# Other phased K pairs for each chunk pair of the input projection, corrected banks in another order, and the rotation on VectorE

## The chip, the cores and the metric

The kernel runs on one core of a Trainium2 chip. The metric is the device time of one execution in microseconds. Three timed runs of the kernel before took 2185.89, 2187.31 and 2187.89 us. Times inside an execution come from a trace of another run, whose zero is the start of its span.

## The reference

Two layers over 256 tokens of width 2048, all in float32. The stage that matters here is the input projection `proj = h @ w_in` and, on two of its six parts, the partial rotation.

```python
def hybrid_mixer(h, layer, w_in, w_o, ...):
    proj = h @ w_in                       # (256, 2048) @ (2048, 6144)
    q_sb, k_sb, v_sb, q_d, k_d, v_d = jnp.split(proj, offs.tolist(), axis=-1)
    o_sb = rms_norm(stick_breaking_attention(q_sb, k_sb, v_sb), sb_out_norm)
    q_d = partial_rope(q_d.reshape(b, s, DIFF_HEADS * 2, DIFF_QK_DIM), pos)
    k_d = partial_rope(k_d.reshape(b, s, DIFF_HEADS * 2, DIFF_QK_DIM), pos)
    o_d = rms_norm(differential_attention(q1, q2, k1, k2, v_d, lam), diff_subln) * (1.0 - lam_init)
    return jnp.concatenate([o_sb, o_d], axis=-1) @ w_o

def partial_rope(x, pos):                 # the first 16 of each 64 are turned, in halves of 8
    rot = jnp.concatenate([x1 * cos - x2 * sin, x2 * cos + x1 * sin], axis=-1)
    return jnp.concatenate([rot, x[..., ROT_DIM:]], axis=-1)

for l in range(DEPTH):
    x = x + rms_norm(hybrid_mixer(rms_norm(x, ...), ...), post_mix_norm[l])
    x = x + rms_norm(swiglu(rms_norm(x, ...), ...), post_ffn_norm[l])
```

## The kernel before

**Split products.** Each float32 matrix is split into a rounded part (hi) and its rest (lo). A product of two blocks is then three matmuls: hi with hi (L1240), hi of the activations with lo of the weights (L1241), and lo of the activations with hi of the weights (L1242). ScalarE (ACT) makes hi of the weights (L402, and in phased K pairs L350, L357 and L376), VectorE (DVE) makes lo (L341). There are six buffers each for hi and lo, and the weights come from HBM in the order in which they are used.

**The input projection.** The 6144 output columns are twelve chunks of 512. They are worked in six pairs of chunks, n = 0 to 5 (`PAIRS`), called pair 1 to pair 6 below. One pair has four banks of 128 tokens x 512 columns that gather in PSUM: two token tiles t0 and t1 for two chunks ca and cb. The code calls them x11 (t0, ca), x12 (t0, cb), x21 (t1, ca) and x22 (t1, cb). The 2048 rows of the weights are eight K pairs (kp), each with two tiles of 128 rows.

**Plain and phased K pairs.** A plain K pair takes eight block products, 24 matmuls (`eight_in`). A phased K pair takes seven, 21 matmuls (`phased`): a scheme of Strassen's kind in which sums of blocks are multiplied. It needs sums of the activations (the tiles `shin` and `slin`, made once for a K pair and layer by `pair_forms`) and sums of the weights, made on DVE for every chunk pair (L349, L351, L355 and L370), and gives seven products with the names g0, t1, t2, t3, then g1, b22, t4. In pair 1 all K pairs are plain. In pairs 2 to 6 the K pairs 0, 1 and 2 are phased (`IN_SEVEN`) and stand first; the plain ones 3 to 7 follow (`IN_PLAIN`). The three forms are made during pair 1.

**The correction.** After the first four products of each phased K pair the banks hold sums that must be set right once: ACT copies x11 (L1207, p1) and x21 (L1210, p7). DVE then makes v1 = x22 - p1 (L1213), x12 + v1 (L1216), x21 - v1 (L1217) and x22 = x12 - p7 (L1218). Only then can the last three products go on: g1 to x11, b22 to x12, t4 to x21. b22 also waits for L1218, which reads x12. The same `phased` serves one part of the output projection.

**The rotation.** `rotate` turns two chunks of q and two of k of the differential heads, for two token tiles: eight times a layer, on a tile of 128 x 128 elements each (8 heads of 16). It is four operations of GpSimd (POOL): L955 (times cosine), L956 and L957 (the exchanged halves times sine) and L958 (their sum). The tokens' rows come from ACT (L1089), and TensorE transposes the turned rows (L1107).

**What sets the order.** Each engine works through its own queue in order. A scheduler puts the instructions into these queues by priority and by what it expects of times; code under `high_priority(offset=URGENT)`, the correction among it, goes ahead of what else is ready. Attention work of finished chunks (`start(...)`) is fed in between the products of the later pairs.

Of the kernel before, what the change touches and what calls it, by code (L numbers as in the profile page):

```python
# [13 lines left out]
ALU = mybir.AluOpType  # L14
# [3 lines left out]
P = 128  # L18
# [4 lines left out]
KT = D // P  # L23
NH = 8
# [61 lines left out]
def weight_order():  # L86

    order = []

    def queue(*blocks):  # L90
        order.append(blocks)
        return len(order) - 1

    def queue_pair(name, l, kp, c):
        return queue((name, l, 2 * kp, c), (name, l, 2 * kp + 1, c))

    roles = {}
# [93 lines left out]
def kernel(  # L191
# [15 lines left out]
    nc = tc.nc  # L207
# [305 lines left out]
    rope_sb = const.tile([P, NT, 32], F32, name="rope_sb")  # L513
# [432 lines left out]
    def rotate(pool, tok, t, nm):  # L946
        v16 = tok.rearrange("p (h d) -> p h d", d=64)[:, :, 0:16]
        ra = pool.tile([P, NH, 16], F32, tag="ra", bufs=1, name=f"ra_{nm}")
        rb = pool.tile([P, NH, 16], F32, tag="rb", bufs=1, name=f"rb_{nm}")

        def table(a, b):
            return rope_sb[:, t, a:b].unsqueeze(1).to_broadcast([P, NH, b - a])

        eng = nc.gpsimd
        eng.tensor_tensor(out=ra, in0=v16, in1=table(0, 16), op=ALU.mult)  # L955
        eng.tensor_tensor(out=rb[:, :, 0:8], in0=v16[:, :, 8:16], in1=table(16, 24), op=ALU.mult)  # L956
        eng.tensor_tensor(out=rb[:, :, 8:16], in0=v16[:, :, 0:8], in1=table(24, 32), op=ALU.mult)  # L957
        eng.tensor_tensor(out=v16, in0=ra, in1=rb, op=ALU.add)  # L958

    def opening(pool, accs, xT, stats, sums_of, settle):  # L960

# [46 lines left out]
        for kp in range(KT // 2):  # L1008
            if kp:
                split(2 * kp)  # L1010
                split(2 * kp + 1)
            if kp + 2 < KT // 2:
                load()
                fetch(2 * kp + 6)
            for part in ((0,), (1,)) if kp == KT // 2 - 1 else (range(NT),):
                eight_in(accs, xT, 0, PAIRS[0], kp, part, kp == 0, kp == KT // 2 - 1, 0)
                if kp == KT // 2 - 1:
                    settle(part[0])
            if 3 <= kp < 7:
# [41 lines left out]
    def mixer_in(pool, l, rs, xT, mix, mixed, began):  # L1061
        heads = {}
        forms, forms_o = {}, {}
        mix_pool[0] = pool.sums

        def sums_of(kp):
            forms[kp] = pair_forms(pool, pool.sums, len(IN_SEVEN), xT, kp, f"in{l}")

        for n, cc in enumerate(PAIRS):
            banks = began[0] if n == 0 and began else four_banks(n == 0, [f"in{l}_{c}_{t}" for t in range(NT) for c in cc])  # L1070
# [50 lines left out]
                opening(pool, banks, xT, first_stats(pool, rs), sums_of, settle)  # L1121
                start(lambdas())
            else:
                kps = IN_PLAIN if n else range(KT // 2)
                ahead = list(KP_O[:2]) if alone else []
                if n:
                    open_sums[0] = True
                    w = pool.tile([P, 4, CW], F32, tag="gpost", bufs=1, name=f"w{l}_{n}")
                    phased(banks, forms, xT, ("in", l, n), IN_SEVEN, [w[:, i, :] for i in range(3)])
                for j, kp in enumerate(kps):  # L1130
                    last = j == len(kps) - 1
                    if n == 0 and 2 <= j < 2 + len(IN_SEVEN):
# [16 lines left out]
                    if ahead and heads[0, 1].keys() >= {"qdone", "kdone"}:  # L1149
                        kp = ahead.pop(0)  # L1150
# [11 lines left out]
    def phased(banks, sums, tiles, key, kps, w):  # L1162

        x11, x12, x21, x22 = banks
# [39 lines left out]
        p1, p7, v1 = w  # L1204
# [6 lines left out]
        products(z, "t2")  # L1211
        with tc.high_priority(offset=URGENT):
            nc.vector.tensor_tensor(out=v1, in0=x22, in1=p1, op=ALU.subtract)  # L1213
        products(z, "t1")
        with tc.high_priority(offset=URGENT):
            nc.vector.tensor_tensor(out=x12, in0=x12, in1=v1, op=ALU.add)  # L1216
            nc.vector.tensor_tensor(out=x21, in0=x21, in1=v1, op=ALU.subtract)  # L1217
            nc.vector.tensor_tensor(out=x22, in0=x12, in1=p7, op=ALU.subtract)  # L1218
# [162 lines left out]
    xT = None  # L1381
# [385 lines left out]
```

## Time and profile before

| what | value |
|---|---|
| three timed runs, median | 2187.31 us |
| the profiled execution | 2184.78 us |
| its span | 2183.0 us |
| its mean granted TensorE clock | 0.998 |
| pairs 2 to 6, layer 0 | 51.7 to 302.0 us |
| pairs 2 to 6, layer 1 | 1136.1 to 1390.0 us |

The profiled execution's own time is 1.8 us longer than the span of its instructions. The stage that the change touches takes some 250 us in each of the two layers. In a row of the trace, a line such as L341 names the line of the kernel that issued the instruction, and `out<-in` its tiles; 128x512 is partitions by elements.

### The profile page before, as it was taken

To read this page: it belongs to the slowest core of one execution; us is meant where nothing else is said; L and a number is where in the kernel's file an instruction comes from. 1 tells how busy PE (TensorE), PEld (TensorE's weight loads), DVE (VectorE), ACT (ScalarE), POOL (GpSimd) and SP (SyncE) were. 2 spreads that over 40 slices of the span, in tenths; PEclk is the share of its full clock that TensorE was granted. 3 is DMA by queue.
4 is the path that set the end of the run, shared out by engine and by line. 5 is a ranking of instruction groups with operands and counts; after the bars stand their busy time and mean duration, and the time that the engine had idled before them with its cause. 6 is when DMAs were issued, how large, how long until landed. Compare 5 with 4: busy or idle time off the path is not lost.

```text
span 2183.0 us, 28896 instructions
## 1 busy us (share of the span) xinstructions
PE 2161.0 (99%) x9902; PEld 1775.8 (81%) x9902; DVE 1979.1 (91%) x2725; ACT 1431.4 (66%) x2157; POOL 249.8 (11%) x238
## 2 busy tenths in 40 slices
PE   9999999999999999999999999999999999999998
PEld 7788888888888888888877778888888888888887
DVE  7988877899999999999898888778999999999997
ACT  7676765766666666666576667657666666676664
POOL 1200000021221220000020100000212212200000
PEclk9999999999999999999999999999999999999999
DMA  8544465487887876767454554655978878767673
GB/s 295 175 173 172 163 218 205 163 306 233 242 262 222 237 233 225 231 228 254 148 197 166 178 184 161 222 192 167 302 237 238 260 225 234 240 219 245 204 266 100
DMA packets 143443, 470.43 MB, mean 215 GB/s; under 512 B 16304, under 2 KB 17328, under 8 KB 142784
## 3 DMA queue, kind: packets, MB, share of 16 engines
q1 hardware_dynamic: 125120, 436.03, 57.3%
q0 software_dynamic: 17600, 32.02, 8.9%
q8 instruction: 77, 1.26, 0.2%
q14 instruction: 70, 0.57, 0.1%
q10 hardware_dynamic: 576, 0.54, 0.1%
HBM read 460.14 MB, written 8.39 MB: 215 GB/s over the span
## 4 chain that ended last, share of the span: by engine, by line
PE 89%; DVE 7%; issue 2%; DMA 1%; ACT 1%; SPq 0%; POOL 0%; DVEq 0%; ACTq 0%; POOLq 0%
PE c L1297 20%; PE in L1241 6%; PE in L1240 6%; PE in L1242 6%; PE dn L1615 4%; PE dn L1616 4%; PE dn L1618 4%; DVE lo L341 3%; PE p L1241 3%; PE c L1240 3%; PE c L1241 3%; PE p L1242 3%; PE c L1242 3%; PE p L1240 3%; PE o L690 2%; PE o L689 2%
## 5 line engine op out<-in xcount | busy, mean ns | idle before, releaser
L341 DVE TENSOR_TENSOR lo<-raw,hi 128x1024 fp32r<-128x1024 f32 (+1 forms) x512 | 597.7, 1186 | 75.8 <-ACT hi L402 49.0
L402 ACT ACTIVATE hi<-raw 128x1024 fp32r<-128x1024 f32 x444 | 455.8, 1057 | 112.4 <-DMA raw<-in_weights_in_turn_dram 64.0
L1297 PE MATMUL c<-hi,xF 128*128 128x512 f32 x1344 | 364.5, 392 | 0.5 <-DVE xF L603 0.5
L1297 PEld LDWEIGHTS c<-hi,xF 128*128 128x128 f32 x1344 | 249.7, 188 | 52.9 <-ACT act L1502 1.4
L296 POOL DMA_DIRECT2D T<-in_weights_in_turn_dram x122 | 107.8, 884 | 1355.9 <-DMA T<-in_weights_in_turn_dram 579.2
L1297 PE MATMUL c<-lo,xF 128*128 128x512 f32 x672 | 207.3, 390 | 0.0
L317 ACT ACTIVATE Th<-T 128x512 fp32r<-128x512 f32 x122 | 77.3, 633 | 193.0 <-DVE T L328 189.0
L317 ACT ACTIVATE Th<-G 128x1024 fp32r<-128x1024 f32 x122 | 129.2, 1059 | 81.7 <-DVE G L329 80.5
L1615 PE MATMUL dn<-hi,jh 128*128 128x512 f32 x416 | 162.0, 389 | 0.0
L1616 PE MATMUL dn<-lo,jh 128*128 128x512 f32 x416 | 161.8, 389 | 0.0
L319 DVE TENSOR_TENSOR Tl<-G,Th 128x1024 fp32r<-128x1024 f32 x122 | 149.2, 1223 | 11.6 <-ACT Th L317 11.6
L319 DVE TENSOR_TENSOR lo<-T,hi 128x1024 fp32r<-128x1024 f32 x122 | 155.1, 1271 | 0.1
L329 DVE TENSOR_TENSOR G<-G,T 128x1024 f32<-128x1024 f32 x122 | 149.0, 1221 | 4.9 <-POOL lo L405 3.1
L402 ACT ACTIVATE hi<-G 128x1024 fp32r<-128x1024 f32 x122 | 129.0, 1058 | 35.9 <-DMA G<-in_weights_in_turn_dram 18.7
L1297 PEld LDWEIGHTS c<-lo,xF 128*128 128x128 f32 x672 | 126.0, 188 | 26.4
L341 DVE TENSOR_TENSOR lo<-G,hi 128x1024 fp32r<-128x1024 f32 x104 | 127.1, 1222 | 10.6 <-ACT hi L402 10.5
L317 ACT ACTIVATE hi<-T 128x1024 fp32r<-128x1024 f32 x122 | 128.3, 1051 | 11.8 <-PE c L1242 8.3
L1618 PE MATMUL dn<-hi,jl 128*128 128x512 f32 x416 | 128.1, 389 | 0.0
L1240 PE MATMUL in<-hi,xT 128*128 128x512 f32 x309 | 123.1, 400 | 2.7 <-DVE in L1217 1.5
L1241 PE MATMUL in<-lo,xT 128*128 128x512 f32 x309 | 120.9, 392 | 0.5 <-DVE lo L1004 0.5
L1242 PE MATMUL in<-hi,xT 128*128 128x512 f32 x309 | 120.5, 390 | 0.0
L1240 PE MATMUL in<-hi,xI 128*128 128x512 f32 x285 | 114.3, 403 | 1.8 <-DVE in L1217 1.8
(462 smaller groups left out, 5057.3 us busy)
## 6 DMA issues: line engine op xcount, KB each, us to landing
raw<-in_weights_in_turn_dram SPq DMA_DIRECT2D x508, 512.0 KB, 4.8
T<-in_weights_in_turn_dram SPq DMA_DIRECT2D x122, 512.0 KB, 5.3
G<-in_weights_in_turn_dram SPq DMA_DIRECT2D x122, 512.0 KB, 5.4
T<-in_weights_in_turn_dram POOLq DMA_DIRECT2D x122, 256.0 KB, 5.8
u<-in_weights_in_turn_dram SPq DMA_DIRECT2D x34, 256.0 KB, 6.0
V<-in_weights_in_turn_dram SPq DMA_DIRECT2D x8, 512.0 KB, 4.4
away_ffn<-x SPq DMA_DIRECT2D x8, 512.0 KB, 7.2
xd<-away_ffn SPq DMA_DIRECT2D x8, 512.0 KB, 8.6
```

The source lines that it names most:

```text
L317: nc.scalar.activation(h, w, AF.Copy)
L319: newest_rest[i] = nc.vector.tensor_tensor(out=l, in0=w, in1=h.bitcast(F32), op=ALU.subtract)
L329: nc.vector.tensor_tensor(out=g, in0=g, in1=t2.unsqueeze(1).to_broadcast([P, 2, CW]), op=ALU.add)
L341: rests.append(nc.vector.tensor_tensor(out=lo, in0=src, in1=hi.bitcast(F32), op=ALU.subtract))
L402: nc.scalar.activation(hi, raw, AF.Copy)
L1240: nc.tensor.matmul(a, sh, hi, start=first, stop=False, skip_group_check=open_sums[0])
L1241: nc.tensor.matmul(a, sh, lo, start=False, stop=False, skip_group_check=open_sums[0])
L1242: return nc.tensor.matmul(a, sl, hi, start=False, stop=last, skip_group_check=open_sums[0])
L1297: nc.tensor.matmul(a, stat[part], w[j][:, kk, :], start=first and kk + n == 0, stop=last and kk == 1 and n == 2)
L1615: nc.tensor.matmul(accs[c, t], sh, hi[:, kk, :], start=first, stop=False, skip_group_check=open_sums[0])
L1616: nc.tensor.matmul(accs[c, t], sh, lo[:, kk, :], start=False, stop=False, skip_group_check=open_sums[0])
L1618: nc.tensor.matmul(accs[c, t], sl, hi[:, kk, :], start=False, stop=last, skip_group_check=open_sums[0])
```

## The change

Three things are changed, and nothing else.

1. `IN_SEVENS` gives each chunk pair its own phased K pairs: none in pair 1, two (0 and 1) in pairs 2 and 3, three in pairs 4 and 5, four in pair 6. That is 14 a layer instead of 15. The forms of K pairs 0 and 1 are still made in pair 1; that of K pair 2 in the plain part of pair 3, and that of K pair 3 in the plain part of pair 5 (`FORMS_AT`). The buffers for forms are four instead of three.
2. In `phased`, x21 is corrected right behind v1, ahead of x12 and x22, and of the last products t4 (which goes to x21) stands ahead of b22 (which goes to x12).
3. `rotate` is three operations of VectorE: both exchanged halves are multiplied in one operation, whose input runs over the halves in reverse.

```diff
-IN_SEVEN = (0, 1, 2)
-IN_PLAIN = (3, 4, 5, 6, 7)
+IN_SEVENS = ((), (0, 1), (0, 1), (0, 1, 2), (0, 1, 2), (0, 1, 2, 3))
+IN_PLAIN = tuple(tuple(kp for kp in range(8) if kp not in mine) for mine in IN_SEVENS)
+FORMS_AT = {(2, 1): 2, (4, 1): 3}
...
-        eng = nc.gpsimd
-        eng.tensor_tensor(out=ra, in0=v16, in1=table(0, 16), op=ALU.mult)
-        eng.tensor_tensor(out=rb[:, :, 0:8], in0=v16[:, :, 8:16], in1=table(16, 24), op=ALU.mult)
-        eng.tensor_tensor(out=rb[:, :, 8:16], in0=v16[:, :, 0:8], in1=table(24, 32), op=ALU.mult)
-        eng.tensor_tensor(out=v16, in0=ra, in1=rb, op=ALU.add)
+        def halves(ap):
+            return ap.rearrange("p h (s e) -> p h s e", s=2)
+
+        sines = halves(rope_sb[:, t : t + 1, 16:32]).to_broadcast([P, NH, 2, 8])
+        nc.vector.tensor_tensor(out=ra, in0=v16, in1=table(0, 16), op=ALU.mult)
+        nc.vector.tensor_tensor(out=halves(rb), in0=halves(v16)[:, :, ::-1, :], in1=sines, op=ALU.mult)
+        nc.vector.tensor_tensor(out=v16, in0=ra, in1=rb, op=ALU.add)
...
-            forms[kp] = pair_forms(pool, pool.sums, len(IN_SEVEN), xT, kp, f"in{l}")
+            forms[kp] = pair_forms(pool, pool.sums, len(IN_SEVENS[-1]), xT, kp, f"in{l}")
...
-                    if n == 0 and 2 <= j < 2 + len(IN_SEVEN):
-                        sums_of(IN_SEVEN[j - 2])
+                    if n == 0 and 2 <= j < 4:
+                        sums_of(j - 2)
+                    if (n, j) in FORMS_AT:
+                        sums_of(FORMS_AT[n, j])
...
             nc.vector.tensor_tensor(out=v1, in0=x22, in1=p1, op=ALU.subtract)
+            nc.vector.tensor_tensor(out=x21, in0=x21, in1=v1, op=ALU.subtract)
         products(z, "t1")
         with tc.high_priority(offset=URGENT):
             nc.vector.tensor_tensor(out=x12, in0=x12, in1=v1, op=ALU.add)
-            nc.vector.tensor_tensor(out=x21, in0=x21, in1=v1, op=ALU.subtract)
             nc.vector.tensor_tensor(out=x22, in0=x12, in1=p7, op=ALU.subtract)
         for two in in_twos(kps):
-            for name in ("g1", "b22", "t4"):
+            for name in ("g1", "t4", "b22"):
                 for kp in two:
                     products(kp, name)
```

After the change most line numbers of this stage are higher: L341 is L342, the correction is L1218 (v1), L1219 (x21), L1222 (x12) and L1223 (x22), the rotation is L959 to L961, and TensorE's three matmuls are L1245 to L1247.

How the instructions stand in DVE's queue, at three places. The first is the start of pair 2 in layer 0. Here raw17, u1_16_0 and the like are weights and their sums; K pair 2, whose weights begin with raw20 before, is the third phased one.

Before:

```order
L341 TENSOR_TENSOR lo17_0_611<-raw17_608,hi17_0_610 128x1024
L341 TENSOR_TENSOR lo17_1_617<-u1_16_0_604,hi17_1_616 128x512
L355 TENSOR_TENSOR raw17_608<-raw17_608,u1_16_0_604 128x512
L351 TENSOR_TENSOR u1_16_1_606<-u1_16_1_606,raw18_623 128x512
L341 TENSOR_TENSOR lo18_0_626<-raw18_623,hi18_0_625 128x1024
L341 TENSOR_TENSOR lo17_1_617<-raw17_608,hi17_1_616 128x512
L355 TENSOR_TENSOR raw18_623<-raw18_623,u1_16_1_606 128x512
L341 TENSOR_TENSOR lo18_1_632<-u1_16_1_606,hi18_1_631 128x512
L349 TENSOR_TENSOR raw20_640<-raw20_640 128x512
```

After:

```order
L342 TENSOR_TENSOR lo17_0_595<-raw17_592,hi17_0_594 128x1024
L959 TENSOR_TENSOR ra_0_6_0_545<-tok0_6_0_543,rope_sb_95 128x128
L960 TENSOR_TENSOR rb_0_6_0_546<-tok0_6_0_543,rope_sb_95 128x128
L356 TENSOR_TENSOR raw17_592<-raw17_592,u1_16_0_588 128x512
L961 TENSOR_TENSOR tok0_6_0_543<-ra_0_6_0_545,rb_0_6_0_546 128x8x16
L342 TENSOR_TENSOR lo17_1_601<-u1_16_0_588,hi17_1_600 128x512
L959 TENSOR_TENSOR ra_0_8_0_552<-tok0_8_0_550,rope_sb_95 128x128
L960 TENSOR_TENSOR rb_0_8_0_553<-tok0_8_0_550,rope_sb_95 128x128
L342 TENSOR_TENSOR lo17_1_601<-raw17_592,hi17_1_600 128x512
```

The rotations of pair 1's chunks (6 and 8) now stand between the rests of the phased weights, and the operations for K pair 2 (raw20) are gone from this pair.

The second place is the correction of pair 3 in layer 0. in0_0_1, in0_0_0 and in0_9_1 are x22, x12 and x21; w0_2 holds p1, p7 and v1; s0_df and mx_df belong to attention.

Before:

```order
L1213 TENSOR_TENSOR w0_2_1052<-in0_0_1_1051,w0_2_1052 128x512
L902 TENSOR_REDUCE mx_df0_0_0_1_1137<-s0_df0_0_0_1_1131 128x2
L1216 TENSOR_TENSOR in0_0_0_1049<-in0_0_0_1049,w0_2_1052 128x512
L1217 TENSOR_TENSOR in0_9_1_1050<-in0_9_1_1050,w0_2_1052 128x512
L1218 TENSOR_TENSOR in0_0_1_1051<-in0_0_0_1049,w0_2_1052 128x512
```

After:

```order
L1218 TENSOR_TENSOR w0_2_1021<-in0_0_1_1020,w0_2_1021 128x512
L921 RECIPROCAL sm_df0_0_0_0_996<-sm_df0_0_0_0_996 128x8
L1219 TENSOR_TENSOR in0_9_1_1019<-in0_9_1_1019,w0_2_1021 128x512
L1222 TENSOR_TENSOR in0_0_0_1018<-in0_0_0_1018,w0_2_1021 128x512
L342 TENSOR_TENSOR lo36_1057<-raw36_1054,hi36_1056 128x1024
L1223 TENSOR_TENSOR in0_0_1_1020<-in0_0_0_1018,w0_2_1021 128x512
```

x21 has moved up by one place, and a rest of a plain weight (lo36) has come between x12 and x22.

The third place is the correction of pair 6 in layer 0. in0_5_1, in0_5_0 and in0_4_1 are x22, x12 and x21; fo0_4 and so0_4 are sums for the output projection.

Before:

```order
L774 TENSOR_TENSOR on_df0_1_1_2597<-o_df0_1_1_2519,ors_df0_1_1_2589 128x512
L1058 TENSOR_TENSOR fo0_4_2742<-mix_df0_0_0_1478 128x256 x2
L1213 TENSOR_TENSOR w0_5_2478<-in0_5_1_2477,w0_5_2478 128x512
L1247 TENSOR_TENSOR so0_4_2745<-fo0_4_2742 128x128
L1216 TENSOR_TENSOR in0_5_0_2475<-in0_5_0_2475,w0_5_2478 128x512
L1217 TENSOR_TENSOR in0_4_1_2476<-in0_4_1_2476,w0_5_2478 128x512
L1218 TENSOR_TENSOR in0_5_1_2477<-in0_5_0_2475,w0_5_2478 128x512
L341 TENSOR_TENSOR lo90_1_2617<-u1_87_0_2479,hi90_1_2616 128x1024
```

After:

```order
L775 TENSOR_TENSOR on_df0_1_1_2583<-o_df0_1_1_2499,ors_df0_1_1_2575 128x512
L342 TENSOR_TENSOR lo88_2_2572<-u1_82_1_2329,hi88_2_2571 128x1024
L1061 TENSOR_TENSOR fo0_4_2763<-mix_df0_0_0_1446 128x256
L342 TENSOR_TENSOR lo89_0_2601<-raw89_2598,hi89_0_2600 128x1024
L1061 TENSOR_TENSOR fo0_4_2763<-mix_df0_0_0_1446 128x256
L1218 TENSOR_TENSOR w0_5_2456<-in0_5_1_2455,w0_5_2456 128x512
L1252 TENSOR_TENSOR so0_4_2766<-fo0_4_2763 128x128
L1219 TENSOR_TENSOR in0_4_1_2454<-in0_4_1_2454,w0_5_2456 128x512
L1222 TENSOR_TENSOR in0_5_0_2453<-in0_5_0_2453,w0_5_2456 128x512
L342 TENSOR_TENSOR lo89_1_2631<-u1_85_0_2457,hi89_1_2630 128x1024
L1223 TENSOR_TENSOR in0_5_1_2455<-in0_5_0_2453,w0_5_2456 128x512
```

Two rests of the now four phased K pairs (lo88_2 and lo89_0) stand ahead of v1, x21 comes ahead of x12, and a third rest (lo89_1) stands between x12 and x22.

More of the change, by code (lines that the diff above doesn't have):

```diff
@@ L112, in weight_order @@
             if n:
-                queue_phase(("in", l, n), "w_in", l, IN_SEVEN, (ca, cb))
-            for kp in IN_PLAIN if n else range(KT // 2):
+                queue_phase(("in", l, n), "w_in", l, IN_SEVENS[n], (ca, cb))
+            for kp in IN_PLAIN[n]:
                 lay["in"][ca, kp] = queue_pair("w_in", l, kp, ca)
@@ L1020, in opening @@
                 next(stats)
-            if 3 <= kp < 3 + len(IN_SEVEN):
-                sums_of(IN_SEVEN[kp - 3])
+            if 3 <= kp < 5:
+                sums_of(kp - 3)
     def first_stats(pool, rs):
@@ L1123, in mixer_in @@
             else:
-                kps = IN_PLAIN if n else range(KT // 2)
+                kps = IN_PLAIN[n]
                 ahead = list(KP_O[:2]) if alone else []
@@ L1128, in mixer_in @@
                     w = pool.tile([P, 4, CW], F32, tag="gpost", bufs=1, name=f"w{l}_{n}")
-                    phased(banks, forms, xT, ("in", l, n), IN_SEVEN, [w[:, i, :] for i in range(3)])
+                    phased(banks, forms, xT, ("in", l, n), IN_SEVENS[n], [w[:, i, :] for i in range(3)])
                 for j, kp in enumerate(kps):
                     last = j == len(kps) - 1
-                    if n == 0 and 2 <= j < 2 + len(IN_SEVEN):
-                        sums_of(IN_SEVEN[j - 2])
+                    if n == 0 and 2 <= j < 4:
+                        sums_of(j - 2)
+                    if (n, j) in FORMS_AT:
+                        sums_of(FORMS_AT[n, j])
                     if n == 0 and 3 <= j < 7:
```

## The prediction

> **What bounds the kernel now.** The page comes first, for the engine that is always busy and for the chain that ended last.
>
> ```profile
> span 2183.0 us, 28896 instructions
> PE 2161.0 (99%) x9902; PEld 1775.8 (81%) x9902; DVE 1979.1 (91%) x2725; ACT 1431.4 (66%) x2157; POOL 249.8 (11%) x238
> PE 89%; DVE 7%; issue 2%; DMA 1%; ACT 1%; SPq 0%; POOL 0%; DVEq 0%; ACTq 0%; POOLq 0%
> ```
>
> TensorE is busy 99% of the span and holds 89% of the chain; DVE holds 7%. So two things can move the time: the number of matmuls, and the short places in which TensorE waits for DVE. The table of waits says where those are (engine, line, what was waited for: us in total, times, longest).
>
> ```profile
> PE in L1241 <- DVE lo L341: 3.8, 4, 1.4
> PE in L1240 <- DVE in L1217: 3.3, 5, 0.9
> PE in L1240 <- ACT hi L357: 1.1, 2, 0.8
> PE in L1240 <- DVE in L1218: 0.8, 1, 0.8
> ```
>
> All four are in the input projection, the only part whose matmuls have the output `in`. They are rests of weights (lo) that come late, and corrected banks (L1217 is x21, L1218 is x22) that come late. Next, the windows of that stage, one for each of the pairs 2 to 6 (n = 1 to 5), layer 0 first. Columns: PE, PEld, DVE, ACT and POOL busy with their instructions, granted clock, DMA share, GB/s.
>
> ```profile
> 51.70:100.30 48.60, 47.66 (x219) 37.22 (x218) 44.69 (x69) 31.07 (x55) 10.71 (x16) 1.00 0.51 179
> 100.30:150.20 49.90, 48.83 (x235) 39.13 (x233) 44.44 (x71) 33.53 (x65) 6.32 (x10) 1.00 0.52 176
> 150.20:197.10 46.90, 46.76 (x232) 38.55 (x231) 39.24 (x57) 31.58 (x63) 2.08 (x4) 1.00 0.49 174
> 197.10:250.70 53.60, 53.60 (x269) 43.76 (x268) 47.13 (x79) 39.80 (x77) 0.00 (x0) 1.00 0.45 157
> 250.70:302.00 51.30, 50.38 (x250) 42.06 (x249) 43.06 (x65) 38.04 (x65) 0.00 (x0) 1.00 0.50 169
> 1136.10:1184.90 48.80, 46.64 (x216) 37.76 (x215) 40.68 (x49) 27.66 (x42) 11.74 (x16) 0.97 0.52 181
> 1184.90:1236.20 51.30, 49.13 (x236) 39.02 (x235) 43.62 (x77) 34.66 (x74) 4.92 (x8) 1.00 0.47 157
> 1236.20:1283.80 47.60, 46.81 (x233) 38.56 (x232) 38.29 (x51) 30.93 (x63) 2.54 (x5) 1.00 0.51 177
> 1283.80:1338.50 54.70, 53.92 (x268) 43.58 (x267) 48.14 (x84) 40.94 (x79) 0.00 (x0) 1.00 0.46 154
> 1338.50:1390.00 51.50, 50.73 (x252) 42.37 (x251) 43.09 (x65) 38.17 (x65) 0.00 (x0) 1.00 0.50 172
> ```
>
> Window less PE is 3.1 us of idle in layer 0 and 6.7 us in layer 1: 9.8 us is all that is visible there. DVE is 80 to 92% busy in each window, so it has some room but little at any one moment. The single waits, from the timeline (start, length, engine, line; idle before it and its releaser in brackets):
>
> ```profile
> 107.91 0.50 PE L1241 MATMUL in<-lo,shin 128*128 128x512 f32 x1 [0.52 <-DVE lo L341]
> 112.96 0.50 PE L1240 MATMUL in<-hi,xT 128*128 128x512 f32 x1 [0.55 <-DVE in L1217]
> 264.10 0.50 PE L1240 MATMUL in<-hi,xT 128*128 128x512 f32 x1 [0.93 <-DVE in L1217]
> 1142.51 0.73 PE L1240 MATMUL in<-hi,shin 128*128 128x512 f32 x2 [0.80 <-ACT hi L357]
> 1144.83 0.79 PE L1241 MATMUL in<-lo,shin 128*128 128x512 f32 x1 [1.36 <-DVE lo L341]
> 1193.34 0.50 PE L1241 MATMUL in<-lo,shin 128*128 128x512 f32 x1 [1.31 <-DVE lo L341]
> 1202.74 0.50 PE L1241 MATMUL in<-lo,shin 128*128 128x512 f32 x1 [0.63 <-DVE lo L341]
> 1249.65 0.50 PE L1240 MATMUL in<-hi,xI 128*128 128x512 f32 x1 [0.79 <-DVE in L1217]
> 1297.73 0.50 PE L1240 MATMUL in<-hi,shin 128*128 128x512 f32 x1 [0.77 <-DVE in L1218]
> 1351.77 0.50 PE L1240 MATMUL in<-hi,xI 128*128 128x512 f32 x1 [0.77 <-DVE in L1217]
> ```
>
> **The change part by part.** Prices first.
>
> ```profile
> 436.45 32.64 PE c L1297 x144
> 1138.14 0.39 PE L1240 MATMUL in<-hi,shin 128*128 128x512 f32 x1
> L341 DVE TENSOR_TENSOR lo<-raw,hi 128x1024 fp32r<-128x1024 f32 x70 | 84.8, 1232 | 18.7 <-ACT hi L402 10.7 <-ACT hi L350 7.8
> L1249 DVE TENSOR_TENSOR sin<-fin x6: 282/287/301, 15.2 to 1121.6; 128x128 f32<-128x128 f32 x6
> L955 POOL TENSOR_TENSOR ra<-tok,rope_sb 128x128 f32<-128x128 f32 x8 | 7.0, 875 | 96.8 <-ACT tok L1089 80.8 <-DMA lams<-in_lambda_q_dram 15.7
> 1134.05 0.81 DVE L355 TENSOR_TENSOR raw<-raw,u 128x512 f32<-128x512 f32 x1
> 1138.71 1.48 DVE L341 TENSOR_TENSOR lo<-raw,hi 128x1024 fp32r<-128x1024 f32 x1
> 1144.70 1.33 DVE L341 TENSOR_TENSOR lo<-u,hi 128x1024 fp32r<-128x1024 f32 x1
> 251.42 1.23 DVE L341 TENSOR_TENSOR lo<-raw,hi 128x1024 fp32r<-128x1024 f32 x1 [1.32 <-ACT hi L350]
> 262.75 0.69 DVE L1216 TENSOR_TENSOR in<-in,w 128x512 f32<-128x512 f32 x1
> 263.35 0.69 DVE L1217 TENSOR_TENSOR in<-in,w 128x512 f32<-128x512 f32 x1
> ```
>
> Matmuls come 32.64 / 144 = 0.227 us apart, though one's record is 0.39 us long; so a wait costs its idle time and 0.16 us more. On DVE an operation of 512 takes 0.69 and the next one starts after 0.60 (262.75 and 263.35); with the same overlap one of 1024 (1.23) takes a step of 1.14.
>
> *Matmuls.* A phased K pair takes 21, a plain one 24. 14 phased a layer instead of 15 is 3 more a layer, 6 x 0.227 = **+1.36 us**. Nothing covers TensorE's own time.
>
> *DVE's load.* A phased K pair costs DVE four additions and two rests of 512 (0.69 each), two rests of 1024 (1.23) and half of one: 7.2 us; a plain one two rests of 1024, 2.5 us. A rotation of three 128x128 operations is 3 x 0.287 = 0.86 us if these run like L1249. One form of tokens (two additions of 256, four of 128, a rest of 512) is about 2.6 us, by the 0.287 and 0.69 and 0.4 between them. For a layer: -4.7 + 2.6 + 8 x 0.86 = +4.8 us in windows that hold 26 to 36 us of free DVE time in all. So only its place counts.
>
> No row shows DVE at a rotation's access (runs of 8, one reversed, a table spread over heads). From below I take the 0.287 of the dense 128x128; from above the 0.69 of L1216, four times the elements. I take 0.29, as the size is the same; the upper end is priced below. [...]
>
> *Pair 2 (n = 1), two phased K pairs, rotations on DVE.* In layer 1 the waits before 1142.51 and 1144.83 cost 0.96 and 1.52 us. Both are for weights of the third phased K pair, which this pair no longer has. While POOL rotates, a rest of 1024 takes 1.48 us instead of 1.23; the 12 operations that start from 1134.05 on and end at 1144.70 (ten of 512, two of 1024) should take 6.0 + 2.3 = 8.3 us by their steps and take 10.65. This stretch of 2.4 us is as much as four rotations of three steps of 0.2 (0.287 less the overlap). So moving them is even, and the third K pair's 4 us ahead of that point are won. Then the clock:
>
> ```profile
> 1144.00:1146.00 2.00, 1.17 (x3) 0.98 (x4) 2.00 (x2) 0.74 (x2) 2.00 (x3) 0.62 0.52 184
> 1146.00:1148.00 2.00, 2.00 (x7) 1.56 (x6) 1.45 (x3) 0.59 (x1) 0.67 (x2) 0.53 0.78 246
> ```
>
> Two waits close together are followed by about 4 us at a granted 0.62 and 0.53, which is 0.76 + 0.94 = 1.7 us lost, some 0.3 of it inside the idle time: 1.4 us. All three terms are 3.9 us; I keep 0.9 for what the rotations put in the way: **-3.0**. [...]
> In layer 0 the waits of pair 2 come to 0.94 us of idle (its window) in some three places, 1.4 us with the hidden part. Four rotations, in a row with rests of weights behind them, must wait for ACT's token rows there: **-0.8**, between 0 and -1.4.
>
> *Pair 3 (n = 2), two phased.* Waits: 0.68 + 0.71 in layer 0, 1.47 + 0.79 and a small one of 0.39 in layer 1. The rests go with the third K pair. New: one rest (lo36, 1.14 of step) stands between x12 and x22 on DVE, so b22 waits about 0.8, and 0.3 for the next rest. Left: 1.1 a layer. 1.39 - 1.1 and 2.65 - 1.1 are 0.3 and 1.55, and with slivers under 0.2 us **-2.1** together.
>
> *Pair 4 (n = 3), still three phased.* x21 is ready one step, 0.60 us, earlier (262.75 to 263.35 shows the step), but TensorE also asks for it earlier, since what stood ahead (one product of a plain pair) has moved behind: **-0.15**.
>
> *Pair 5 (n = 4).* L1218 was waited for (0.93 in layer 1); now t4 lies between and covers x12 and x22: **-1.25** in both layers.
>
> *Pair 6 (n = 5), four phased.* Ahead of the correction DVE gets four additions (2.4 us of steps), a rest of 1024 and two of 512 (1.14 + 1.2) and half a rest (0.55) more, 5.3 us. From this go 0.6 for x21's earlier place and some 2.1 us in which DVE idles there now (1.32 before 251.42, the others under 0.4 each): x21 is 2.6 us later. TensorE asks 9 matmuls later (12 more first products, one g1 fewer ahead), 2.05 us. The waits before 264.10 and 1351.77 grow by 0.55 each: **+1.1**. Without that idle time it would be 2 us more a layer.
>
> The o stage's phased part gets the same new order; no wait there is in the table, so 0, within 0.6 us either way. Extra forms (pairs 3 and 5) lie in plain phases, at 0 while DVE idles there; without cover 2.7 us a layer.
>
> Sum: 1.36 - 3.0 - 0.8 - 2.1 - 0.15 - 1.25 + 1.1 = **-4.8 us**. The profiled execution took 2184.78 us (span 2183.0), so its like would take 2180.0. The timed runs have a median of 2187.31, 2.5 more; the forecast for them is **2182.5**.
>
> **Rivals.** *A: the waits move.* DVE's work is in order, so a rotation at its head that waits for ACT holds every rest behind it, and x22 behind lo36 does the same. For it: 44.69 of 48.60 busy in pair 2 of layer 0. Against: TensorE's buffer of six rests. If pair 2 wins only 1.0 in layer 1 and nothing in layer 0, and pair 3 half: 1.36 - 1.0 - 1.05 - 1.4 + 1.1 = -1.0, 2186.3.
> *B: nearly all waits go.* -9.8 visible, -1.6 for some ten hidden parts, +1.36: -10, 2177. For it: most named rows belong to K pairs that are gone. Against: pair 6 keeps its wait.
> *C, slower: a rotation at 0.69 an operation.* It then takes 2.07 us. In pair 2 of layer 0 that is 44.69 - 4.7 + 4 x 2.07 = 48.3 us of DVE, and 49.3 with a quarter of its present 3.9 us of idle, which waits for ACT. TensorE needs 48.6 + 0.7 for three more matmuls - 1.4 of waits = 47.9, so DVE is the bound. Pair 2's gain of 3.8 goes, the rests end 1.3 us later in each layer, and two clusters of waits bring the low clock, 1.4 each: -4.8 + 3.8 + 2.6 + 2.8 = +4.4, 2191.7. It decides from about 0.5 us an operation. Against: 0.287 at this size.
> *D: the change doesn't do what it says*, and K pairs or rotations stay in place: 0. The rows of DVE shown with the change speak against it.
>
> **How the numbers follow.** About 0.2%, 4.4 us, is what can be told from no change. Forecast (-7 to -2.5) 0.55, of which 0.37 lies beyond 4.4; A 0.22; B 0.13; C 0.08; D 0.02. Faster 0.37 + 0.13 = 0.50, same 0.18 + 0.22 + 0.02 = 0.42, slower 0.08. The range takes in forecast and A, and most of B: 2177.5 to 2188.5; it leaves out C and B's far half.
>
> **What would show it.** Right: POOL empty in pairs 2 to 4; no wait for a rest and a clock of 1.00 near 1144; waits for L1223 in pair 3 of about 0.8; waits for L1219 of 1.5 to 1.7 in pair 6; rotation rows of 0.28 to 0.30. Wrong: rotation rows over 0.5, a wait of pair 6 over 2.5, or rests that are late in pair 2 of either layer.

## The result, and the profile after

Eight timed runs of the changed kernel took 2176.78 to 2181.79 us, median 2179.83; eight of the kernel before took 2183.79 to 2187.89, median 2186.28. The ratio is 0.997, with a 95% interval of 0.9959 to 0.9981: 6.5 us faster, between 4.2 and 9.0. The forecast was 4.8 faster. The forecast time, 2182.5 us, is 2.7 above the measured median; 1.0 of that is in its base, as the median of the kernel before is 2186.28 over eight runs and was 2187.31 over the three known then. The profiled execution took 2177.17 us.

The page of the changed kernel: the span, the engines, and the chain that ended last.

```profile
span 2175.5 us, 28819 instructions
PE 2156.7 (99%) x9908; PEld 1775.2 (82%) x9908; DVE 1980.9 (91%) x2771; ACT 1427.9 (66%) x2151; POOL 205.3 (9%) x174
PE 86%; DVE 8%; DMA 3%; issue 1%; ACT 1%; DVEq 0%; SPq 0%; ACTq 0%
```

TensorE is still the bound, with 99% of the span; DVE's total has hardly moved (1979.1 before), and POOL has lost the 44 us of the rotations. Where the 7.5 us of span went, the page doesn't say. TensorE's table of waits, with the lines of the input projection:

```profile
PE in L1245 <- DVE in L1219: 3.7, 3, 1.3
PE in L1245 <- DVE in L1223: 1.1, 2, 0.5
PE in L1246 <- DVE lo L342: 0.6, 1, 0.6
```

Rests of weights (lo) were waited for four times, 3.8 us in all; now once, 0.6 us. What is left in pairs 2 to 6 is mainly the corrected banks: x21 (L1219) three times, x22 (L1223) twice. Below are the windows of pairs 2 to 6 in the trace of the changed kernel, layer 0 first, with the columns as before. They are cut at the first matmul of each pair, and pair 6 ends with the first matmul of the output projection; the windows in the prediction start 0.7 us later, and those of pair 6 end 0.5 to 0.8 us earlier.

```profile
50.28:98.60 48.32, 46.41 (x219) 37.41 (x218) 40.25 (x65) 27.73 (x43) 0.00 (x0) 1.00 0.56 193
98.60:148.52 49.92, 49.38 (x240) 39.67 (x239) 44.38 (x86) 33.69 (x73) 0.00 (x0) 1.00 0.48 162
148.52:195.23 46.71, 46.71 (x233) 38.42 (x231) 38.83 (x56) 31.38 (x63) 0.00 (x0) 1.00 0.51 180
195.23:249.00 53.77, 53.45 (x268) 43.67 (x267) 49.91 (x91) 40.63 (x78) 0.00 (x0) 1.00 0.49 167
249.00:301.46 52.46, 51.22 (x259) 42.86 (x257) 47.76 (x72) 40.69 (x68) 0.00 (x0) 1.00 0.48 161
1134.99:1180.63 45.64, 45.64 (x219) 37.35 (x218) 34.19 (x48) 25.91 (x40) 0.00 (x0) 1.00 0.56 192
1180.63:1230.58 49.95, 49.41 (x239) 39.66 (x238) 44.37 (x86) 33.76 (x73) 0.00 (x0) 1.00 0.46 162
1230.58:1277.28 46.70, 46.70 (x232) 38.42 (x231) 38.89 (x56) 31.32 (x63) 0.00 (x0) 1.00 0.52 181
1277.28:1330.93 53.65, 53.43 (x268) 43.67 (x267) 50.00 (x91) 40.67 (x78) 0.00 (x0) 1.00 0.48 167
1330.93:1383.39 52.46, 51.21 (x258) 42.85 (x257) 47.76 (x72) 40.71 (x68) 0.00 (x0) 1.00 0.48 161
```

POOL is empty. Layer 1 has no idle time at all in pairs 2 and 4, and 2.0 us in all five (6.7 before). Layer 0 has 4.0 us, more than the 3.1 before: 1.9 of it in pair 2. So the idle time that went was in layer 1. The waits that remain, from the timeline:

```profile
59.37 0.49 PE L1245 MATMUL in<-hi,xT 128*128 128x512 f32 x1 [1.19 <-DVE in L1219]
61.09 0.50 PE L1246 MATMUL in<-lo,xT 128*128 128x512 f32 x1 [0.62 <-DVE lo L342]
108.75 0.50 PE L1245 MATMUL in<-hi,shin 128*128 128x512 f32 x1 [0.54 <-DVE in L1223]
265.92 0.50 PE L1245 MATMUL in<-hi,xT 128*128 128x512 f32 x1 [1.24 <-DVE in L1219]
1190.78 0.50 PE L1245 MATMUL in<-hi,shin 128*128 128x512 f32 x1 [0.54 <-DVE in L1223]
1347.87 0.50 PE L1245 MATMUL in<-hi,xI 128*128 128x512 f32 x1 [1.25 <-DVE in L1219]
```

The first two are new, in pair 2 of layer 0, and the second of them is a late rest, which the prediction had named as a sign of being wrong. The new operations, by the profile's rows for one line each (nanoseconds, least/median/most):

```profile
L959 DVE TENSOR_TENSOR ra<-tok,rope_sb x16: 266/287/296, 47.8 to 1230.8; 128x128 f32<-128x128 f32 x16
L960 DVE TENSOR_TENSOR rb<-tok,rope_sb x16: 272/283/288, 48.0 to 1231.0; 128x128 f32<-128x128 f32 x16
L961 DVE TENSOR_TENSOR tok<-ra,rb x16: 274/284/295, 48.8 to 1231.3; 128x128 f32<-128x128 f32 x16
```

The reversed halves and the table spread over heads cost VectorE nothing extra here: medians of 0.283 to 0.287 us, where the dense additions of 128x128 (L1249) took 0.285 to 0.288 in the kernel before.

### The profile page after: what moved, and what is told of

It reads as the page before. It is cut to its first block, busy times and chain, and to the rows that moved or that the text cites. A ratio compares the mean times of both kernels' runs of the same rounds, so it can differ in the third digit from the quotient of the medians.

```text
span 2175.5 us, 28819 instructions
## 1 busy us (share of the span) xinstructions
PE 2156.7 (99%) x9908; PEld 1775.2 (82%) x9908; DVE 1980.9 (91%) x2771; ACT 1427.9 (66%) x2151; POOL 205.3 (9%) x174
## 4 chain that ended last, share of the span: by engine, by line
PE 86%; DVE 8%; DMA 3%; issue 1%; ACT 1%; DVEq 0%; SPq 0%; ACTq 0%
PE c L1302 20%; PE in L1245 5%; PE in L1246 5%; PE in L1247 5%; PE dn L1620 4%; PE dn L1621 4%; PE dn L1623 4%; DVE lo L342 3%; PE p L1246 3%; PE c L1245 3%; PE c L1246 3%; PE c L1247 3%; PE p L1247 3%; PE p L1245 3%; DMA raw<-in_weights_in_turn_dram 2%; PE o L689 2%
## 5 line engine op out<-in xcount | busy, mean ns | idle before, releaser
L342 DVE TENSOR_TENSOR lo<-raw,hi 128x1024 fp32r<-128x1024 f32 (+1 forms) x508 | 596.1, 1191 | 61.5 <-ACT hi L403 44.8
L1302 PEld LDWEIGHTS c<-hi,xF 128*128 128x128 f32 x1344 | 249.8, 188 | 53.4 <-ACT act L1507 1.9
L342 DVE TENSOR_TENSOR lo<-G,hi 128x1024 fp32r<-128x1024 f32 x104 | 126.8, 1219 | 10.2 <-ACT hi L403 10.1
L1245 PE MATMUL in<-hi,xT 128*128 128x512 f32 x314 | 124.7, 400 | 3.7 <-DVE in L1219 2.4
L1247 PE MATMUL in<-hi,xT 128*128 128x512 f32 x314 | 122.2, 390 | 0.0
L1245 PE MATMUL in<-hi,xI 128*128 128x512 f32 x290 | 116.0, 401 | 1.3 <-DVE in L1219 1.3
```

What stands on the lines that cost most here:

```text
L342: rests.append(nc.vector.tensor_tensor(out=lo, in0=src, in1=hi.bitcast(F32), op=ALU.subtract))
L1245: nc.tensor.matmul(a, sh, hi, start=first, stop=False, skip_group_check=open_sums[0])
L1247: return nc.tensor.matmul(a, sl, hi, start=False, stop=last, skip_group_check=open_sums[0])
L1302: nc.tensor.matmul(a, stat[part], w[j][:, kk, :], start=first and kk + n == 0, stop=last and kk == 1 and n == 2)
```

## Experiments

The length of a pair, from its first matmul to that of the next, can repeat well between executions of one kernel: pair 2 of layer 1 took 48.81, 48.76 and 48.78 us in three traces of the kernel before. Not all do (pair 6 of layer 1 took 52.66, 52.37 and 53.41), and the total varies by some 5 us from run to run. So a kernel is read by both, its time and its pairs, and a difference of under 1 us in one pair counts only where several traces agree. Theory 1 is that of the prediction: VectorE's own work decides, and the third phased K pair was too much of it in pairs 2 and 3. Theory 2: POOL and VectorE hinder each other while POOL rotates. Theory 3: the order of the corrected banks.

### Each part alone

`kpairs_alone` has the new `IN_SEVENS`, the rest as before:

```diff
-IN_SEVEN = (0, 1, 2)
...
+IN_SEVENS = ((), (0, 1), (0, 1), (0, 1, 2), (0, 1, 2), (0, 1, 2, 3))
...
+FORMS_AT = {(2, 1): 2, (4, 1): 3}
...
```

> Only the phased K pairs of each chunk pair are changed (2, 2, 3, 3, 4); rotation on POOL and the order of the banks as before. Theory 1 (the third phased K pair's work on VectorE is what made weights late in pairs 2 and 3 of layer 1): 3 to 5 us faster than before; pair 2 of layer 1 falls from 48.8 to 46.5 us or less, the granted clock near 1144 us is 1.00. Theory 2 (POOL and VectorE hinder each other during the rotations, that made them late): 0 to 1 us faster, pair 2 of layer 1 stays above 47.5 us and the clock still falls.

`rotation_alone` has only the new `rotate`:

```diff
-        eng = nc.gpsimd
...
+        nc.vector.tensor_tensor(out=ra, in0=v16, in1=table(0, 16), op=ALU.mult)
...
```

> Only the rotation moves to VectorE. Theory 1: 0.5 us faster (0 to 1.5), as four rotations cost VectorE as much as the stretch that goes; pair 2 of layer 1 stays above 47.5 us with a late rest of weights. Theory 2: 3 us faster or more, pair 2 of layer 1 at 46.5 us or less.

`order_alone` has only the new order:

```diff
+            nc.vector.tensor_tensor(out=x21, in0=x21, in1=v1, op=ALU.subtract)
         products(z, "t1")
...
-            nc.vector.tensor_tensor(out=x21, in0=x21, in1=v1, op=ALU.subtract)
...
-            for name in ("g1", "b22", "t4"):
+            for name in ("g1", "t4", "b22"):
```

> Only the corrected banks come in another order (x21 first, t4 ahead of b22). Theory 1 and 2: 1.3 us faster (0.5 to 2), mostly pair 5 of layer 1 (54.7 us before, 53.7 now). Theory 3 (the order of the banks is most of the gain): 3 us faster or more, with pairs 4 and 6 of both layers each 0.5 us shorter.

`all_again` is the changed kernel.

> The changed kernel again, beside its parts on one chip: 6.5 us faster than before (5 to 8). If the three parts only add up, it is their sum; if it is more, the parts help each other.

### Each part taken back out of the changed kernel

`no_rotation` has the four POOL operations again:

```diff
-        nc.vector.tensor_tensor(out=ra, in0=v16, in1=table(0, 16), op=ALU.mult)
...
+        eng = nc.gpsimd
...
```

> The changed kernel with the rotation back on POOL. Theory 1 (VectorE's own order decides; a rotation on VectorE holds the correction of pair 2 in layer 0 back): 0.5 to 1.5 us faster than the changed kernel, so 6.5 to 8 faster than before; pair 2 of layer 0 takes 46.8 us (48.3 in the changed kernel), that of layer 1 46.1 (45.7). Theory 2 (POOL and VectorE hinder each other): 1 us or more slower than the changed kernel, in pairs 2 and 3 of both layers.

`no_order` has the old order of the banks:

```diff
-            for name in ("g1", "t4", "b22"):
+            for name in ("g1", "b22", "t4"):
...
```

> The changed kernel with the old order of the corrected banks. If the parts add up: 1.2 us slower than the changed kernel (5 faster than before), with pair 5 of layer 1 at 54.9 us (53.7) and pair 4 at 47.0. If the new order only helps where the waits of pair 2 were: the same as the changed kernel.

`no_kpairs` has three phased K pairs in each of pairs 2 to 6:

```diff
-IN_SEVENS = ((), (0, 1), (0, 1), (0, 1, 2), (0, 1, 2), (0, 1, 2, 3))
+IN_SEVENS = ((), (0, 1, 2), (0, 1, 2), (0, 1, 2), (0, 1, 2), (0, 1, 2))
...
-FORMS_AT = {(2, 1): 2, (4, 1): 3}
+FORMS_AT = {}
...
```

> The changed kernel with the old K pairs (three phased in each of pairs 2 to 6). If the parts add up: 2.4 us faster than before (1 to 3.5), 4 slower than the changed kernel, the rests of weights in pairs 2 and 3 late again (pair 3 of layer 1 near 51 us). If rotation and order carry the gain: 5 or more faster than before.

### What these seven show

Ratios are to the kernel before in runs on the same chip; pairs are in us, from the traces; "2 / 0" is pair 2 of layer 0.

| kernel | ratio, 95% interval | 2 / 0 | 2 / 1 | 3 / 1 | 4 / 1 | 5 / 1 | pairs 2 to 6, both layers |
|---|---|---|---|---|---|---|---|
| before (3 traces, mean) | 1 | 48.6 | 48.8 | 51.1 | 47.2 | 54.5 | 506.5 |
| kpairs_alone | 0.9978, 0.9969 to 0.9987 | 46.8 | 46.1 | 50.6 | 47.0 | 54.9 | 502.1 |
| rotation_alone | 0.9994, 0.9985 to 1.0003 | 48.2 | 47.4 | 50.9 | 46.6 | 55.4 | 505.7 |
| order_alone | 0.9993, 0.9985 to 1.0002 | 48.7 | 47.6 | 51.1 | 47.0 | 53.5 | 505.5 |
| `order_look`, the same kernel again | one run | 48.6 | 47.6 | 51.7 | 47.7 | 53.3 | 506.2 |
| the changed kernel | 0.997, 0.9959 to 0.9981 | 48.3 | 45.7 | 50.0 | 46.7 | 53.7 | 499.6 |
| all_again | 0.9974, 0.9963 to 0.9985 | 48.3 | 45.8 | 50.0 | 46.7 | 53.6 | 500.4 |
| no_rotation | 0.9963, 0.9949 to 0.9976 | 46.9 | 45.9 | 50.2 | 49.7 | 53.7 | 502.2 |
| no_order | 0.9971, 0.9961 to 0.9981 | 48.3 | 46.5 | 50.0 | 47.2 | 54.2 | 501.7 |
| no_kpairs | 0.9977, 0.9968 to 0.9986 | 48.7 | 47.4 | 50.6 | 47.4 | 53.3 | 502.5 |

*K pairs.* Alone they bring 4.8 us, as theory 1 expected, and pair 2 of layer 1 falls to 46.1 with POOL still rotating: the third K pair's work is a cause of the late rests there, and theory 2 can't be the only one. This is TensorE in layer 0 of `kpairs_alone`; the third K pair's weights are no longer waited for, and what is left in pair 2 is small:

```profile
56.68 0.50 PE L1244 MATMUL in<-lo,shin 128*128 128x512 f32 x1 [0.24 <-DVE lo L342]
62.28 0.50 PE L1244 MATMUL in<-lo,shin 128*128 128x512 f32 x1 [0.25 <-DVE lo L342]
```

But the parts do not add up as that theory had it. Rotation and order together (`no_kpairs`) bring 5.0 us, not the 2.4 expected, and the K pairs on top of them only some 1 us more (0.9977 against 0.997 and 0.9974, with intervals that overlap; 2 to 3 us by the pairs). The late rests of pair 2 in layer 1 are gone there too, with three phased K pairs; one is left in pair 3 of layer 1 (TensorE in `no_kpairs`):

```profile
1144.89 0.49 PE L899 MATMUL s_df<-kT,qT 64*128 64x128 f32 x2 [0.32 <-ACT kT L1111]
1188.84 0.50 PE L1246 MATMUL in<-lo,shin 128*128 128x512 f32 x1 [0.66 <-DVE lo L342]
```

So the same waits can be taken away in two ways, and whoever comes second finds less: the three parts alone add up to 7.6 us, and `all_again`, measured beside them, brings 5.7 (inside the expected 5 to 8). The late rest of pair 2 in layer 1 needed both the third K pair's work and the rotations on POOL, since it goes when either goes.

*Scores.* The idle time isn't all. TensorE also works the scores of attention (`s_df`) between the products, and what these take depends on how they are strewn. Their busy time in pair 2 of layer 0, in the kernel before and in the changed one, and in pair 2 of layer 1 in `rotation_alone` (columns: PE, PEld, DVE and ACT, clock, DMA share, GB/s):

```profile
51.04:99.60 48.56, 2.61 (x18) 1.63 (x18) 1.91 (x4) 3.18 (x16) 1.00 0.51 179
50.28:98.60 48.32, 1.16 (x16) 0.97 (x16) 1.89 (x4) 1.41 (x8) 1.00 0.56 193
1136.21:1183.60 47.39, 2.39 (x16) 1.62 (x16) 1.91 (x4) 1.16 (x6) 1.00 0.57 189
```

Sixteen scores in one row keep TensorE busy for 1.16 us; in groups of two to ten the same sixteen take 2.39. In pair 2 of layer 0 they come in one row in all seven traces with two phased K pairs there, and strewn, 18 or 20 of them at 2.60 to 3.04 us, in all seven with three. In pair 2 of layer 1 they are strewn only in `rotation_alone` and `no_kpairs`. So of the 1.8 us that the K pairs alone bring in pair 2 of layer 0, about 1.4 is the place of the scores. From `no_kpairs` to the changed kernel the scores of pairs 2 and 3 fall by 3.1 us, while the idle time of pairs 2 to 6 grows from 5.1 to 6.0; what the K pairs add there is not a wait that goes. No experiment moved the scores alone.

*Rotation.* Alone, it is 1.3 us faster by the ratio, with an interval that reaches no change. In time `rotation_alone` is where theory 1 had it, but not in its pair: pair 2 of layer 1 took 47.4 us, not over 47.5 with a late rest. Its idle time fell from 2.1 to 0.4 us and its clock stayed at 1.00, so the relief that theory 2 speaks of is there (a rest of 1024 takes 1.23 us in that stretch, and 1.22 or 1.23 in that of the changed kernel, against up to 1.48 beside POOL in the kernel before), and the strewn scores above take 1.2 us of it back. In the changed kernel the rotation costs: pair 2 of layer 0 takes 46.8 and 46.9 us in the two kernels with the new K pairs that rotate on POOL, and 48.3 in all with them that rotate on VectorE. In the trace of the changed kernel VectorE stands still at the first of four rotations until ACT has written its token rows, their twelve operations go in among the weights, and then it corrects x12 ahead of x21, which TensorE waits for:

```profile
47.80 0.29 DVE L959 TENSOR_TENSOR ra<-tok,rope_sb 128x128 f32<-128x128 f32 x1 [1.75 <-ACT tok L1092]
58.03 0.69 DVE L1222 TENSOR_TENSOR in<-in,w 128x512 f32<-128x512 f32 x1
58.63 0.69 DVE L1219 TENSOR_TENSOR in<-in,w 128x512 f32<-128x512 f32 x1
```

`no_rotation` has x21 first there, and a rest of weights before it; TensorE waits 0.82 us for a tile that POOL turns, and the pair is shorter all the same. It is about as fast as the changed kernel (2177.59 us, 0.9963, with intervals that overlap), although its profile lost 3 us in pair 4 of layer 1; the last section says to what.

*Order.* Alone 1.5 us faster, again with an interval that reaches no change, as expected in size; pair 5 of layer 1 falls by 1.1 us, as expected. Taking it out of the changed kernel costs 1 to 2 us in the pairs and nothing that the times can tell. Theory 3 falls.

### A best of both, and pair 6

`rotation_by_layer` rotates on POOL in layer 0 and on VectorE in layer 1:

```diff
+        if nm[0] == "0":
+            eng = nc.gpsimd
+            eng.tensor_tensor(out=ra, in0=v16, in1=table(0, 16), op=ALU.mult)
...
+            return
```

> The changed kernel, but layer 0 rotates on POOL and layer 1 on VectorE. Theory 1 (on VectorE the rotation holds back pair 2 of layer 0 and helps pair 2 of layer 1): pairs 2 to 6 take 249.9 us in layer 0 and 248.4 in layer 1, 1.3 us faster than the changed kernel, 7.5 to 8 faster than before. Theory 2 (the pairs come out as they do by chance of the scheduler's order): layer 0 does not come out at 249.9, and there is no gain over the changed kernel.

Measured: 2177.23 us against 2185.86, ratio 0.9958 (0.9946 to 0.9971), 8.6 us by the medians. Pairs 2 to 6 of layer 0 took 249.8 us, with pair 2 at 46.7: theory 1 holds there. Those of layer 1 took 250.4, not 248.4, all of it by pair 4 (48.6 instead of 46.7). It has the best median, but its interval overlaps with the changed kernel's, so that it beats that one is likely by its layer 0 and not shown by its times.

`pair6_three` has a fourth phased K pair nowhere:

```diff
-IN_SEVENS = ((), (0, 1), (0, 1), (0, 1, 2), (0, 1, 2), (0, 1, 2, 3))
+IN_SEVENS = ((), (0, 1), (0, 1), (0, 1, 2), (0, 1, 2), (0, 1, 2))
...
-FORMS_AT = {(2, 1): 2, (4, 1): 3}
+FORMS_AT = {(2, 1): 2}
```

> The changed kernel with three phased K pairs in pair 6. As predicted (a fourth costs 0.55 us of wait a layer and saves 3 matmuls, 0.68): pair 6 is 0.1 us longer than in the changed kernel and its wait for x21 shorter by 0.5; the total the same within 0.5 us. If the fourth costs nothing: pair 6 is 0.7 us longer in each layer, 1.4 in all. If the fourth is what delays VectorE (rival C's kind): pair 6 gets shorter.

Measured: 2179.73 us, ratio 0.9974 (0.9964 to 0.9983). Pair 6 took 53.35 us in both layers, 0.7 to 0.9 longer than in the changed kernel's two traces (52.45 to 52.66), which is the case in which the fourth costs nothing. The wait for x21 in it:

```profile
263.54 0.50 PE L1245 MATMUL in<-hi,xT 128*128 128x512 f32 x1 [1.20 <-DVE in L1219]
1347.16 0.50 PE L1245 MATMUL in<-hi,xI 128*128 128x512 f32 x1 [1.20 <-DVE in L1219]
```

With four phased K pairs it is 1.24 and 1.25, and 1.40 and 1.45 in the second trace. So the fourth costs 0.05 to 0.25 us of wait and saves its three matmuls. That the wait is longer than before the change goes with the order, in which TensorE asks for t4 earlier: `order_alone`, with three phased K pairs, has it too, at 1.16 to 1.19 us in both of its traces. Before the change it was 0.93 and 0.77 us in the trace of the prediction, and 0.34 to 1.56 in the other two; with rotation and order, in `no_kpairs`, it is 0.80 and 1.06. So the order's share isn't sharp.

```profile
264.48 0.50 PE L1243 MATMUL in<-hi,xT 128*128 128x512 f32 x1 [1.18 <-DVE in L1217]
1351.05 0.50 PE L1243 MATMUL in<-hi,xI 128*128 128x512 f32 x1 [1.16 <-DVE in L1217]
```

### The clock

`before_again` and `before_look` are the kernel before, `order_look` is `order_alone`, each profiled once more.

> The kernel before once more, for its profile. Theory A (two waits of 0.8 and 1.3 us close together lower the clock every time): granted clock near 0.6 for some 3 us in pair 2 of layer 1, which takes 48.8 us. Theory B (whether they do depends on when they come, as in the kernel with the new order alone, where the same two waits left the clock at 1.00): the clock may stay at 1.00, and the pair then takes 47.6 us.

> The kernel with the new order alone, looked at again for its clock. Before it had the two waits of pair 2 in layer 1 (0.80 and 1.34 us) at a clock of 1.00. If its clock stays at 1.00 again, something in this kernel keeps it; if it falls to about 0.6 for 3 us, the fall comes in some executions and not in others, and pair 2 takes 48.8 us instead of 47.6.

> The kernel before, looked at a third time for its clock; twice it fell to 0.62 and 0.53 behind the two waits. If by chance: it may stay at 1.00, with pair 2 of layer 1 at 47.6 us. If by the waits: 0.6 again, 48.8 us.

TensorE and the windows in the second trace of the kernel before (granted clock is the third number from the end):

```profile
1144.61 0.74 PE L1240 MATMUL in<-hi,shin 128*128 128x512 f32 x2 [0.79 <-ACT hi L357]
1146.92 0.79 PE L1241 MATMUL in<-lo,shin 128*128 128x512 f32 x1 [1.34 <-DVE lo L341]
```

```profile
1143.05:1146.46 3.41, 1.74 (x7) 0.79 (x5) 3.41 (x5) 2.31 (x4) 3.25 (x5) 1.00 0.02 5
1146.46:1149.88 3.42, 2.96 (x7) 2.38 (x8) 2.87 (x4) 0.96 (x2) 2.30 (x3) 0.50 0.75 253
```

And the same two views of `order_look`:

```profile
1144.77 0.73 PE L1243 MATMUL in<-hi,shin 128*128 128x512 f32 x2 [0.81 <-ACT hi L358]
1147.08 0.50 PE L1244 MATMUL in<-lo,shin 128*128 128x512 f32 x1 [1.35 <-DVE lo L342]
```

```profile
1143.16:1146.57 3.41, 1.76 (x7) 0.82 (x5) 3.41 (x5) 2.26 (x4) 3.25 (x5) 1.00 0.02 5
1146.57:1149.98 3.41, 2.90 (x13) 2.36 (x14) 3.41 (x4) 1.01 (x2) 2.36 (x3) 1.00 0.74 262
```

The waits are the same to 0.02 us, and the clock falls in one kernel and not in the other: 7 matmuls fit into the second window of the one, 13 into that of the other. It fell in all three traces of the kernel before and in neither of the two of `order_alone`. Pair 2 of layer 1 took 48.8 us in the three and 47.6 in the two, so the fall costs 1.2 us. So theory A falls: these waits do not lower the clock every time. Chance at even odds would give three and none in 1 of 32 cases.

In all three traces of the kernel before the fall lasts 3.41 us, and in the 3.41 us ahead of it TensorE was busy for 1.61, 1.74 and 1.66 us. In `order_look` the stretch of that length which holds both waits is busy for 1.76 us, and the clock stayed at 1.00. In `order_alone` it stayed there too, over these two stretches, which between them hold both waits (0.80 and 1.34 us):

```profile
1141.10:1144.51 3.41, 2.85 (x13) 2.04 (x11) 3.41 (x4) 2.21 (x3) 3.25 (x5) 1.00 0.33 131
1144.51:1147.93 3.42, 1.84 (x7) 1.22 (x8) 3.42 (x4) 2.33 (x5) 3.34 (x4) 1.00 0.24 69
```

What parts the two kernels is not shown: no experiment moved the waits alone.

## Why the prediction came out as it did

The sum had the right sign and most of the size: 4.8 us forecast, 6.5 measured, and the pairs 2 to 6 shortened by 6.5 (506.5 to 500.0, mean of the traces), 5.8 of it in layer 1. By its terms, each with its matmuls (3 more in pairs 2 and 3, 3 fewer in pair 6, 0.68 us each time):

| term | forecast | measured |
|---|---|---|
| pair 2, layer 0 | -0.1 | -0.3 |
| pair 2, layer 1 | -2.3 | -3.1 |
| pair 3, both | -0.7 | -1.1 |
| pair 4, both | -0.15 | -0.7 |
| pair 5, both | -1.25 | -1.1 |
| pair 6, both | -0.3 | -0.3 |

*Pair 2, layer 1.* The mechanism was right: weights of the third K pair were the wait. The size was 0.8 short, because the 0.9 that was kept back for rotations in the way did not come: the window has no idle time. Of the 3.9 us of waits and clock that the prediction added up, 3.8 went (3.1 and the 0.68 of three more matmuls). What the prediction called even, four rotations against the stretch that goes, was better than even there: `rotation_alone` has no late rest in this pair. The step from two waits close together to a low clock was too simple: in `order_alone` waits of 0.80 and 1.34 us left it at 1.00. The clock term itself, 1.4 predicted, measured 1.2. The kernel before shows the fall three times, with no wait there longer than 1.36 us.

*Pair 2, layer 0.* Right by luck. The term was 0.8 us of waits that go. They grew instead, from 0.9 us of idle time to 1.9, with the late rest that was to be a sign of being wrong. The K pairs alone give 1.8 us there, most of it the scores in one row, for which the prediction had no term, and the rotation on VectorE takes 1.5 back. That is rival A's mechanism, at one place: the queue stands 1.75 us for ACT at a rotation.

*Pair 3.* b22 does wait for x22, by 0.54 us where 0.8 was said, in layer 0 behind lo36, and the further 0.3 is absent; so the gain came out 0.4 us larger.

*Pair 4.* Undersized by 0.55. It was argued that TensorE asks for x21 earlier too, so that the wait stays; it is gone in both layers (46.71 of 46.71 and 46.70 of 46.70 busy). But the wait of 0.79 us that the prediction read was that of one execution: in the other two traces of the kernel before it is 0.15 and 0.20, and `order_alone` has 0.21 and 0.90 there. What took it away is not shown.

*Pair 5.* Right: t4 between the correction and b22 covers x12 and x22; taking the order out brings a wait for L1223 back in both layers (0.89 and 0.63 us) and lengthens the pair by 0.5 in layer 1. The term had 0.3 us more than the row it named (0.93) and named nothing for it; layer 0 showed no idle time in that trace, and a wait of 0.8 for x22 in the other two.

*Pair 6.* Right in the sum, wrong in the cause: against the trace of the prediction the wait grew by 0.3 us in layer 0 and 0.5 in layer 1, but little of it by the fourth phased K pair, which `pair6_three` prices at 0.05 to 0.25; most of it goes with the new order, as far as the traces agree. It stayed under the 1.5 to 1.7 that were to be seen.

*Bounds.* The rotation at 0.28 us an operation (rows of 266 to 296 ns) shuts out rival C, whose point was 0.5, and bears out the 0.29 that was taken from the dense 128x128. Rival B went too far: 6.0 of 9.8 us of visible idle time are still there. VectorE's free time in the windows of the prediction is 32 and 40 us a layer, not 26 to 36; nothing in the sum hangs on it.

## What to carry to other kernels

Where an engine that feeds TensorE is nearly full (here VectorE, busy for 91% of the span), it is worth spending a few matmuls in the stage in which that engine is behind, and saving them where it is not: six more matmuls (1.4 us) went with 4.8 us less in all. Before two remedies are combined, each should be tried alone and each taken out: here each of two ways brought 5 us and both together 5.7 to 6.5, and one of the three edits cost 1.5 us at one place. Moving work from a slow engine to a fast one that others wait for (here from a median of 0.80 us for L955 on POOL to 0.29 for L959 on VectorE) is paid for by whatever stands behind it in the queue (in pair 2 of layer 0, 48.3 us against 46.8 and 46.9), so it has to be judged place by place. And when an edit changes an engine's order, its idle time is not the whole account: here the same sixteen scores took 1.16 or 2.39 us.

## What the runs showed of the hardware beyond that

The clock: two waits of 0.8 and 1.35 us with three matmuls between them went with 3.41 us at a granted 0.50, in three traces of three of one kernel and in none of two of another. In the 3.41 us ahead of the fall TensorE was busy for 1.61 to 1.74 us; in `order_look` such a stretch with 1.76 was followed by none. What decides it is not shown.

Where a gain was lost, a transfer had come late. Three kernels lost 1.8 to 3 us in pair 4 of layer 1, in their profiled execution, where the changed kernel lost nothing. In `pair6_three`, VectorE waits for a weight of the third phased K pair of that pair, and TensorE then for x21; VectorE first, then TensorE:

```profile
1221.96 0.69 DVE L350 TENSOR_TENSOR raw<-raw 128x512 f32<-128x512 f32 x1 [1.18 <-DMA raw<-in_weights_in_turn_dram]
```

```profile
1245.55 0.50 PE L1245 MATMUL in<-hi,xI 128*128 128x512 f32 x1 [1.57 <-DVE in L1219]
```

The changed kernel runs the same operation without a wait:

```profile
1219.48 0.69 DVE L350 TENSOR_TENSOR raw<-raw 128x512 f32<-128x512 f32 x1
```

`no_rotation` and `rotation_by_layer` show the same wait for a transfer, of 2.11 and 0.86 us. With the wait for the first of these K pairs, which the changed kernel has too, VectorE waits 3.5, 4.2 and 3.6 us for weights of this pair in the three kernels, and 1.7 and 1.1 in the two traces of the changed one. That this delay becomes the wait for x21 (1.53 to 1.57 us in the three, none in the changed kernel) is read from the order of VectorE's queue; it wasn't tried with an earlier transfer. Each of the three was profiled once. A single kernel does vary at this place, by 0.6 us between the traces of the kernel before (47.6, 46.9 and 47.0) and 0.7 between those of `order_alone`; whether the larger delay comes with these kernels or with single executions is open.
